# Prompt attention, one head at a time or two: scores, transposed weights and one eviction in shared banks

## The chip, the cores and the metric

The kernel runs on one core of a Trainium2 chip. The metric is device time in microseconds, the median of several executions. The engines are TensorE (PE; its weight loads are shown as PEld), VectorE (DVE), ScalarE (ACT), GpSimd (POOL) and SyncE (SP), which issues most of the transfers.

## The reference, cut to what matters

One inference step of a one-layer decoder: 1024 prompt tokens and 8 sample tokens go through gated branches (dilated window attention A, a convolution B, attention into 256 memory tokens M) and a channel mixer that retrieves experts. The change touches the prompt's part of A and M:

```python
# A: three head groups (window, dilation) = (128,1), (512,4), (2048,16), four heads each
s = jnp.einsum('brnqhd,brnkhd->brnhqk', qb, kk) * (HEAD_DIM ** -0.5)
s = jnp.where(mask[None, None, :, None], s, -jnp.inf)      # band of the window, blocks of 128
p, lse = softmax_lse(s)
o = jnp.einsum('brnhqk,brnkhd->brnhqd', p, vv)
...
# M: four heads, 256 memory tokens
s = jnp.einsum('bshd,bmhd->bhsm', qm, mk) * (HEAD_DIM ** -0.5)
p = jax.nn.softmax(s, axis=-1)
return jnp.einsum('bhsm,bmhd->bshd', p, mv)
```

All is float32; the outputs are the prompt's and the samples' rows and new cache rows.

## The kernel before, in words

The program prepares the memory keys and values, then runs `front` and `tail` for the first half of the prompt (512 tokens and the 8 samples), again for the second half, and last the dense expert stage `peer_dense`, beside which `peer_gather` fetches the experts of the last three token blocks by indirect DMA (L981). The dense stage begins near 1900 us.

Inside `front(hf, ...)` the projections write queries, keys and values to scratch in DRAM. A pool `mix` then holds everything from attention to the gated merge. For each of three groups and four packs of 128 queries (L357 to L388) the loads of queries, keys and values of this pack (and, where there is one, of the pack before) go to tiles `ld`. With a previous pack a head has 256 keys (`nk`), else 128. Per head: TensorE transposes keys and query into slot `t0` (L380), ScalarE evicts them to `kq` (L382), and `unit` does the rest. Memory attention (L420 to L439) calls the same `unit`, always with 256 keys. There are 24 packs of window attention (15 with 256 keys a head, 9 with 128) and 8 blocks of memory attention, so 128 calls of `unit`: 92 with 256 keys and 36 with 128.

`unit` does, for one head: a score matmul into slot `t1` (L319; it shows as two instructions, since the matmul is float32), a masked reduction on VectorE (L321, output S and the negated maximum), an exponential on ScalarE with its sum (L325), transposes of S into slot `t2` (L328), one eviction to ST by ScalarE (L330), and matmuls with the values into the head's columns of `po` (L332). The slots `t0`, `t1`, `t2` are one PSUM bank each (512 float32 a partition), with one buffer. S and ST are tiles of 256 columns in two buffers, `kq` has two.

In the first half alone, `sample_scores` (L390) reduces rows of the caches with VectorE (L405), and `sample_mix` (L441) multiplies cached values. Both load tiles of 128 x 512 float32 (256 KB) into a ring `sld` of eight buffers: keys at L396, broadcast queries at L400, values at L529. All these loads, attention's and the weights' go through SP's queue in one order.

The convolution of the first half runs 30 taps a channel block on VectorE (L575). Gates (L645) and the convolution's input (L559) are the bulk of TensorE's work here.

No order is written by hand. A planner takes the instructions in program order as priorities, with a simulated time line, and lays down one order for each engine and its queue; on the chip each engine keeps that order and waits at semaphores.

Of the kernel before, what the change touches and what calls it, by code (L numbers as in the profile page):

```python
# [9 lines left out]
F32 = mybir.dt.float32  # L10
# [6 lines left out]
OP = mybir.AluOpType  # L17
# [4 lines left out]
P = 128  # L22
# [24 lines left out]
def peer_trunk(tc, I, O):  # L47
# [11 lines left out]
    with contextlib.ExitStack() as es:  # L59
# [198 lines left out]
        def front(hf, keep, wp):  # L258
# [53 lines left out]
            with tc.tile_pool(name=f"mix{hf}", bufs=1) as mx, banks(f"mix{hf}"):  # L312
                LD = 10 if hf == 0 else 6


                def unit(qT, kT, nk, vs, mask, po, h, negm, den, name):

                    pS = t_tile(f"pS_{name}", 1)
                    nc.tensor.matmul(pS[:, :nk], qT, kT, start=True, stop=True)  # L319
                    S = mx.tile([P, 256], F32, tag="S", bufs=2, name=f"S_{name}")  # L320
                    nc.vector.tensor_tensor_reduce(  # L321
                        out=S[:, :nk], in0=pS[:, :nk], in1=mask, scale=-SCALE, scalar=BIG,
                        op0=OP.add, op1=OP.min, accum_out=negm,
                    )
                    nc.scalar.activation(S[:, :nk], S[:, :nk], AF.Exp, scale=-1.0, bias=negm, accum_out=den)  # L325
                    pT = t_tile(f"pT_{name}", 2)
                    for j in range(nk // P):
                        nc.tensor.transpose(pT[:, j * P : (j + 1) * P], S[:, j * P : (j + 1) * P], ident)  # L328
                    ST = mx.tile([P, 256], F32, tag="ST", bufs=2, name=f"ST_{name}")
                    nc.scalar.copy(ST[:, :nk], pT[:, :nk])  # L330
                    for j in range(nk // P):
                        nc.tensor.matmul(  # L332
                            po[:, h * P : (h + 1) * P], ST[:, j * P : (j + 1) * P], vs[j][:, h * P : (h + 1) * P],
                            start=j == 0, stop=j == nk // P - 1,
                        )

                def ld_tile(name):
                    return mx.tile([P, 520], F32, tag="ld", bufs=LD, name=name)

                def sld_tile(name):  # L340
                    return mx.tile([P, 512], F32, tag="sld", bufs=8, name=name)


                def rows_of(scr, g, pk, hh, c0, c1):
# [12 lines left out]
                for g in range(3):  # L357
                    for pk in range(4):
                        nm = f"{hf}{g}{pk}"

                        def ld(scr, which, hh, pp, cc, nm=nm, g=g):
                            t = ld_tile(f"w{which}{nm}")
                            nc.sync.dma_start(t[:, :512], rows_of(scr, g, pp, hh, cc, cc + 512))
                            return t

                        prev = prev_of(g, pk)
                        q = ld(qscr, "q", hf, pk, 512 * g)
                        ks = [ld(kscr, "kp", prev[0], prev[1], 0)] if prev else []
                        ks.append(ld(kscr, "ko", hf, pk, 0))
                        vs = [ld(vscr, "vp", prev[0], prev[1], 0)] if prev else []  # L370
                        vs.append(ld(vscr, "vo", hf, pk, 0))
                        nk = P * len(ks)
                        mask = masks[:, 1 if g == 2 else 0, 256 - nk : 256]
                        po = o_tile(f"wo{nm}")
                        ao = mx.tile([P, 520], F32, tag="ao", bufs=2, name=f"wao{nm}")
                        for h in range(4):
                            hs = slice(h * P, (h + 1) * P)
                            pt = t_tile(f"wT{nm}{h}", 0)
                            for j, src in enumerate(ks + [q]):
                                nc.tensor.transpose(pt[:, j * P : (j + 1) * P], src[:, hs], ident)  # L380
                            kq = mx.tile([P, 384], F32, tag="kq", bufs=2, name=f"kq{nm}{h}")
                            nc.scalar.copy(kq[:, : nk + P], pt[:, : nk + P])  # L382
                            unit(
                                kq[:, nk : nk + P], kq[:, :nk], nk, vs, mask, po, h,
                                ao[:, 512 + h : 513 + h], ao[:, 516 + h : 517 + h], f"w{nm}{h}",
                            )
                        nc.scalar.copy(ao[:, :512], po)
                        nc.sync.dma_start(rows_of(oscr[g], g, pk, hf, 0, 520), ao)  # L388
# [31 lines left out]
                for c0, n, row, rb in blocks[:4]:  # L420
# [1 line left out]
                    nc.sync.dma_start(qt[:, :512], qscr[row : row + n, 1536:2048])  # L422
                    po = o_tile(f"mo{hf}{c0}")
                    nm = small.tile([P, 8], F32, tag="nmd", name=f"mnmd{hf}{c0}")
                    for h in range(4):
                        pt = t_tile(f"mqT{hf}{c0}{h}", 0)
                        nc.tensor.transpose(pt[:, :P], qt[:, h * P : (h + 1) * P], ident)
                        kq = mx.tile([P, 384], F32, tag="kq", bufs=2, name=f"mqTs{hf}{c0}{h}")
                        nc.scalar.copy(kq[:, :P], pt[:, :P])
                        unit(  # L430
                            kq[:, :P], kTm[:, h, :], 256, (vm[:, 0, :], vm[:, 1, :]), zmask, po, h,
                            nm[:, h : h + 1], nm[:, 4 + h : 5 + h], f"m{hf}{c0}{h}",
                        )
                    nc.vector.reciprocal(nm[:, 4:8], nm[:, 4:8])
                    a = mx.tile([P, 520], F32, tag="ao", bufs=2, name=f"ma{hf}{c0}")
# [810 lines left out]
```

## Time and profile before

| | us |
|---|---|
| median of 3 runs | 3703.09 (3703.05 to 3704.65) |
| the profiled execution | 3695.24 |
| its span, first to last instruction | 3693.1 |
| TensorE busy | 3429.9 (93%) |
| VectorE busy | 2899.1 (78%) |
| ScalarE busy | 1499.6 (41%), 3519 instructions |

The rows further down come from this one execution. A row of a stage gives the busy time of each engine inside it and the mean granted clock of TensorE as a part of full speed (1.00 is 2.4 GHz; 0.5 would be 1.2 GHz all the time). A row of a wait names the waiting engine and line, the one that released it, the sum of the idle time, how often, and the longest.

### The profile page before, as it was taken

How to read it: one execution, taken by the hardware profiler on the slowest of the kernel's cores; microseconds unless marked ns; L12 is line 12 of the kernel's file. 1: busy time of each engine (PE TensorE's matmuls, PEld its weight loads, DVE VectorE, ACT ScalarE, POOL GpSimd, SP SyncE). 2: the span in 40 equal slices, each digit the busy share in tenths (PEclk: the TensorE clock that was granted, in tenths of full speed). 3: DMA queues.
4: the chain of work that ended last, by engine and by line, in shares of the span. 5: the costliest groups of instructions: out<-in, count | busy, mean ns of one | idle time of the engine just before them, and what ended most of it. 6: DMA issues, size and time to landing. Idle time of an engine off the chain costs nothing.

```text
span 3693.1 us, 55182 instructions
## 1 busy us (share of the span) xinstructions
PE 3429.9 (93%) x19969; PEld 3011.5 (82%) x19969; DVE 2899.1 (78%) x6275; ACT 1499.6 (41%) x3519; POOL 565.7 (15%) x398
## 2 busy tenths in 40 slices
PE   8987999898889989887899999999999999999998
PEld 6766989697677778676798888888989888898987
DVE  4358555499998656779988888887988888798988
ACT  6553552235755554344443333332333333233332
POOL 0000000000000000000012323322323332233332
PEclk9997999999999999998799999999999999999999
DMA  5467455423355546753668988888988988888987
GB/s 180 136 199 259 154 184 183 154 86 119 103 186 189 177 157 211 246 188 131 224 233 314 338 312 330 310 318 309 336 328 324 342 315 304 308 327 318 334 329 279
DMA packets 338454, 902.09 MB, mean 244 GB/s; under 512 B 32588, under 2 KB 140276, under 8 KB 285436
## 3 DMA queue, kind: packets, MB, share of 16 engines
q1 hardware_dynamic: 281732, 487.49, 39.7%
q0 software_dynamic: 56448, 411.07, 29.2%
q8 instruction: 157, 2.57, 0.3%
q14 instruction: 117, 0.96, 0.1%
HBM read 804.09 MB, written 94.83 MB: 243 GB/s over the span
## 4 chain that ended last, share of the span: by engine, by line
PE 31%; issue 30%; DVE 14%; DMA 13%; POOL 11%; ACT 2%; SPq 0%; POOLq 0%; DVEq 0%; ACTq 0%
POOL uv L981 11%; DMA uv<-in_uv,idxB 4%; PE pg L175 2%; PE pg L174 2%; PE pg L176 2%; PE pG L1057 2%; PE pG L1056 2%; DMA vr<-in_v_tab 1%; PE p_q L175 1%; PE p_q L176 1%; DMA wko<-kscr 1%; PE p_q L174 1%; DMA uv<-in_uv,idxS 1%; PE pa L174 1%; PE pa L176 1%
## 5 line engine op out<-in xcount | busy, mean ns | idle before, releaser
L981 POOL DMA_INDIRECT uv<-in_uv,idxB x384 | 555.8, 1448 | 1553.2 <-DVE gacc L995 1226.1
L174 PE MATMUL pa<-h2Ah,uh 128*128 128x320 f32 x2048 | 633.7, 310 | 2.2 <-ACT uh L158 2.2
L176 PE MATMUL pa<-h2Ah,ul 128*128 128x320 f32 x2048 | 631.9, 310 | 2.3 <-DVE ul L159 2.2
L175 PE MATMUL pa<-h2Al,uh 128*128 128x320 f32 x2048 | 633.2, 309 | 0.0
L985 DVE CUSTOM_DVE_ANT_0 uv<-uv,gh 128x1024 f32<-128x1024 f32 x392 | 478.5, 1222 | 138.2 <-DMA uv<-in_uv,idxB 119.9
L174 PE MATMUL pv<-vh,hh 128*128 128x512 f32 x1280 | 480.5, 396 | 44.3 <-ACT vh L158 28.4
L995 DVE SCALAR_TENSOR_TENSOR gacc<-uv,av,gacc 128x1024 f32<-128x1024 f32 x392 | 502.5, 1282 | 17.5 <-ACT av L993 12.6
L175 PE MATMUL pv<-vl,hh 128*128 128x512 f32 x1280 | 505.2, 395 | 9.3 <-DVE vl L159 9.3
L176 PE MATMUL pv<-vh,hl 128*128 128x512 f32 x1280 | 499.9, 393 | 0.0
L174 PEld LDWEIGHTS pa<-h2Ah,uh 128*128 128x128 f32 x2048 | 385.7, 188 | 6.9 <-ACT uh L158 2.4
L176 PEld LDWEIGHTS pa<-h2Ah,ul 128*128 128x128 f32 x2048 | 385.1, 188 | 5.4 <-DVE ul L159 2.8
L175 PEld LDWEIGHTS pa<-h2Al,uh 128*128 128x128 f32 x2048 | 385.4, 188 | 3.3 <-issue 0.9
L158 ACT CAST vh<-vr 128x512 fp32r<-128x512 f32 x256 | 157.2, 619 | 422.0 <-DMA vr<-in_v_tab 238.1
L174 PEld LDWEIGHTS pv<-vh,hh 128*128 128x128 f32 x1280 | 242.7, 190 | 99.0 <-ACT vh L158 40.0
L175 PEld LDWEIGHTS pv<-vl,hh 128*128 128x128 f32 x1280 | 243.6, 190 | 61.0 <-DVE vl L159 12.9
L176 PEld LDWEIGHTS pv<-vh,hl 128*128 128x128 f32 x1280 | 243.4, 190 | 50.0
L981 POOL DMA_INDIRECT uv<-in_uv,idxS x8 | 9.2, 1149 | 1556.3 <-ACT co L739 1513.2
L159 DVE TENSOR_TENSOR vl<-vr,vh 128x512 fp32r<-128x512 f32 x256 | 175.6, 688 | 77.0 <-ACT vh L158 76.5
L174 PE MATMUL pg<-hTh,wh_g 128*128 128x260 f32 (+1 forms) x576 | 192.9, 335 | 0.0
L175 PE MATMUL pg<-hTl,wh_g 128*128 128x260 f32 (+1 forms) x576 | 192.4, 334 | 0.0
L176 PE MATMUL pg<-hTh,wl_g 128*128 128x260 f32 (+1 forms) x576 | 192.3, 334 | 0.0
L990 ACT ACTIVATE av<-av 128x2 f32<-128x2 f32 x196 | 39.9, 204 | 375.3 <-DVE av L985 374.8
(558 smaller groups left out, 7651.3 us busy)
## 6 DMA issues: line engine op xcount, KB each, us to landing
ur<-in_uT SPq DMA_DIRECT2D x128, 512.0 KB
vr<-in_v_tab SPq DMA_DIRECT2D x256, 256.0 KB
gscr<-stg SPq DMA_DIRECT2D x20, 2048.0 KB
Gt<-gscr SPq DMA_DIRECT2D x32, 1280.0 KB
wr_g<-in_w_col SPq DMA_DIRECT2D x48, 512.0 KB
wr_q<-in_w_in SPq DMA_DIRECT2D x24, 512.0 KB
wr_u<-in_w_col SPq DMA_DIRECT2D x16, 512.0 KB
wr_pq<-in_w_col SPq DMA_DIRECT2D x16, 512.0 KB
```

Of the source, the lines that this page charges most:

```text
L158: nc.scalar.copy(hi, raw)
L159: nc.vector.tensor_tensor(lo, raw, hi.bitcast(F32), op=OP.subtract)
L174: nc.tensor.matmul(out, ah, bh, start=start, stop=False)
L175: nc.tensor.matmul(out, ah, bl, start=False, stop=False)
L176: nc.tensor.matmul(out, al, bh, start=False, stop=stop)
L981: nc.gpsimd.indirect_dma_start(out=uv, out_offset=None, in_=I["uv"], in_offset=bass.IndirectOffsetOnAxis(ap=col, axis=0),)
L985: nc.vector.tensor_tensor_reduce(out=uv[:, 0:D], in0=uv[:, 0:D], in1=h2, scale=1.0, scalar=0.0, op0=OP.mult, op1=OP.add, accum_out=av[:, s ...
L990: nc.scalar.activation(av, av, AF.Gelu_apprx_tanh)
L995: nc.vector.scalar_tensor_tensor(acc, uv[:, D:], av[:, j : j + 1], acc, op0=OP.mult, op1=OP.add)
L1056: nc.tensor.matmul(pG[:, q], o2[:, a, :, q], wh[:, a, :, q], start=True, stop=False)
L1057: nc.tensor.matmul(pG[:, q], o2[:, a, :, q], wl[:, a, :, q], start=False, stop=True)
```

## The change

`unit` becomes `pair`, for two heads. One tile of `t1` holds both heads' scores side by side, one tile S and one ST of 512 columns hold both heads, one tile of `t2` takes all transposes (two or four), and one eviction moves them. The query and key tiles of a head are made by a function that `pair` calls for each head (`window_qk`, `memory_qk`), so the transposes and the eviction to `kq` now stand inside the loop over the two heads. The score matmul, the reduction and the exponential stay one for each head. The transposes of both heads follow the second head's exponential in the program. The ring `sld` has seven buffers instead of eight.

```diff
-                def unit(qT, kT, nk, vs, mask, po, h, negm, den, name):
+                def pair(qkT, nk, vs, mask, po, h0, negm, den, name):
 
                     pS = t_tile(f"pS_{name}", 1)
-                    nc.tensor.matmul(pS[:, :nk], qT, kT, start=True, stop=True)
-                    S = mx.tile([P, 256], F32, tag="S", bufs=2, name=f"S_{name}")
-                    nc.vector.tensor_tensor_reduce(
-                        out=S[:, :nk], in0=pS[:, :nk], in1=mask, scale=-SCALE, scalar=BIG,
-                        op0=OP.add, op1=OP.min, accum_out=negm,
-                    )
-                    nc.scalar.activation(S[:, :nk], S[:, :nk], AF.Exp, scale=-1.0, bias=negm, accum_out=den)
+                    S = mx.tile([P, 512], F32, tag="S", bufs=2, name=f"S_{name}")
                     pT = t_tile(f"pT_{name}", 2)
-                    for j in range(nk // P):
+                    ST = mx.tile([P, 512], F32, tag="ST", bufs=2, name=f"ST_{name}")
+                    for q in range(2):
+                        qT, kT = qkT(h0 + q)
+                        nc.tensor.matmul(pS[:, q * nk : (q + 1) * nk], qT, kT, start=True, stop=True)
+                        nc.vector.tensor_tensor_reduce(
+                            out=S[:, q * nk : (q + 1) * nk], in0=pS[:, q * nk : (q + 1) * nk], in1=mask, scale=-SCALE,
+                            scalar=BIG, op0=OP.add, op1=OP.min, accum_out=negm(h0 + q),
+                        )
+                        nc.scalar.activation(
+                            S[:, q * nk : (q + 1) * nk], S[:, q * nk : (q + 1) * nk], AF.Exp, scale=-1.0,
+                            bias=negm(h0 + q), accum_out=den(h0 + q),
+                        )
+                    for j in range(2 * nk // P):
                         nc.tensor.transpose(pT[:, j * P : (j + 1) * P], S[:, j * P : (j + 1) * P], ident)
-                    ST = mx.tile([P, 256], F32, tag="ST", bufs=2, name=f"ST_{name}")
-                    nc.scalar.copy(ST[:, :nk], pT[:, :nk])
-                    for j in range(nk // P):
-                        nc.tensor.matmul(
-                            po[:, h * P : (h + 1) * P], ST[:, j * P : (j + 1) * P], vs[j][:, h * P : (h + 1) * P],
-                            start=j == 0, stop=j == nk // P - 1,
-                        )
+                    nc.scalar.copy(ST[:, : 2 * nk], pT[:, : 2 * nk])
+                    for q in range(2):
+                        hs = slice((h0 + q) * P, (h0 + q + 1) * P)
+                        for j in range(nk // P):
+                            js = slice(q * nk + j * P, q * nk + (j + 1) * P)
+                            nc.tensor.matmul(po[:, hs], ST[:, js], vs[j][:, hs], start=j == 0, stop=j == nk // P - 1)
...
-                    return mx.tile([P, 512], F32, tag="sld", bufs=8, name=name)
+                    return mx.tile([P, 512], F32, tag="sld", bufs=7, name=name)
...
-                        for h in range(4):
+                        def window_qk(h, nm=nm, ks=ks, q=q, nk=nk):
                             hs = slice(h * P, (h + 1) * P)
                             pt = t_tile(f"wT{nm}{h}", 0)
...
+                            return kq[:, nk : nk + P], kq[:, :nk]
+
+                        for h0 in (0, 2):
+                            pair(
+                                window_qk, nk, vs, mask, po, h0, lambda h, ao=ao: ao[:, 512 + h : 513 + h],
+                                lambda h, ao=ao: ao[:, 516 + h : 517 + h], f"w{nm}{h0}",
                             )
```

Memory attention is rewritten in the same way with `memory_qk`.

## Rows read from the trace of the kernel before

**Rows 1.** The page's first part: engines' busy time, share of the span, instructions.

```profile
PE 3429.9 (93%) x19969; PEld 3011.5 (82%) x19969; DVE 2899.1 (78%) x6275; ACT 1499.6 (41%) x3519; POOL 565.7 (15%) x398
```

**Rows 2.** Busy time by stage: us, engines busy (instructions), PE clock, DMA share, GB/s.

```profile
240.00:360.00 120.00, 92.95 (x544) 78.41 (x543) 99.90 (x471) 45.28 (x132) 0.00 (x0) 0.81 0.88 289
360.00:490.00 130.00, 128.70 (x1050) 126.34 (x1051) 69.10 (x156) 74.34 (x216) 0.00 (x0) 1.00 0.48 146
...
1260.00:1340.00 80.00, 64.33 (x347) 51.24 (x344) 43.93 (x75) 38.07 (x75) 0.00 (x0) 0.87 0.40 142
1340.00:1480.00 140.00, 136.95 (x845) 118.26 (x844) 84.98 (x163) 72.28 (x171) 0.00 (x0) 0.98 0.59 200
...
1900.00:3694.00 1794.00, 1731.16 (x9568) 1566.46 (x9567) 1517.14 (x1979) 567.31 (x1305) 547.87 (x378) 0.99 0.87 319
```

**Rows 3.** Score matmuls of window attention, first half, second half: count, ns, first and last start.

```profile
L319 PE MATMUL pS_w<-kq x96: 270/275/796, 244.8 to 432.5; 128*128 128x128 f32 x72, 128*128 128x256 f32 x24
...
L319 PE MATMUL pS_w<-kq x96: 377/379/716, 1054.0 to 1362.1; 128*128 128x256 f32 x96
```

**Rows 4.** Waits of TensorE, 240 to 500 us: waiter, releaser, us, times, longest.

```profile
PE pS_w L319 <- DVE wao L321: 20.1, 13, 5.7
...
PE pT_w L328 <- ACT S_w L325: 0.9, 2, 0.6
PE mo L332 <- ACT ST_m L330: 0.5, 1, 0.5
```

**Rows 5.** The same of the second half, 1080 to 1480 us.

```profile
PE wT L380 <- DMA wkp<-kscr: 17.2, 5, 7.9
...
PE wo L332 <- ACT ST_w L330: 2.0, 4, 0.9
...
PE pT_w L328 <- ACT S_w L325: 0.5, 1, 0.5
```

**Rows 6.** Groups of evictions, 240 to 1480 us: line, operation, shapes, count | busy, mean ns | idle.

```profile
L330 ACT COPY ST_w<-pT_w 128x256 f32<-128x256 f32 x60 | 22.5, 375 | 18.7 <-PE pT_w L328 18.0
...
L387 ACT COPY wao<-wo 128x512 f32<-128x512 f32 x24 | 14.0, 585 | 8.9 <-PE wo L332 8.9
...
L330 ACT COPY ST_m<-pT_m 128x256 f32<-128x256 f32 x32 | 12.0, 376 | 24.0 <-PE pT_m L328 23.7
...
L330 ACT COPY ST_w<-pT_w 128x128 f32<-128x128 f32 x36 | 9.7, 269 | 7.1 <-PE pT_w L328 6.9
```

**Rows 7.** Waits of VectorE, 240 to 500 us.

```profile
DVE skw L405 <- DMA sqw<-qscr: 12.8, 4, 7.6
...
DVE S_m L321 <- PE pT_m L328: 3.8, 1, 3.8
...
DVE skm L405 <- DMA sqm<-qscr: 2.5, 3, 1.7
...
DVE S_w L321 <- PE pT_w L328: 1.6, 2, 0.9
```

**Rows 8.** Time line around 343 us: start, us, engine, line, operation [idle before, releaser].

```profile
343.61 0.29 DVE L405 CUSTOM_DVE_ANT_0 skw<-skw,sqw 128x128 f32<-128x128 f32 x1 [7.56 <-DMA sqw<-qscr]
...
345.13 0.28 DVE L321 CUSTOM_DVE_ANT_0 S_w<-pS_w,c_masks 128x128 f32<-128x128 f32 x1
...
345.48 0.79 PE L319 MATMUL pS_w<-kq 128*128 128x128 f32 x2 [5.70 <-DVE wao L321]
```

**Rows 9.** Waits of SP's DMA queue, 240 to 360 us.

```profile
SPq L396 <- DVE s_allm L405: 7.0, 7, 2.1
...
SPq L396 <- DVE s_allw L405: 4.6, 4, 1.8
```

**Rows 10.** Waits of TensorE in the dense stage, 1900 to 3694 us.

```profile
PE pv L174 <- ACT vh L158: 28.4, 11, 5.4
PE pv L174 <- DVE dacc L1124: 12.9, 4, 7.4
PE pv L175 <- DVE vl L159: 9.3, 8, 4.1
```

More of the change, by code (lines that the diff above doesn't have):

```diff
@@ L382, in front @@
                             nc.scalar.copy(kq[:, : nk + P], pt[:, : nk + P])
-                            unit(
-                                kq[:, nk : nk + P], kq[:, :nk], nk, vs, mask, po, h,
-                                ao[:, 512 + h : 513 + h], ao[:, 516 + h : 517 + h], f"w{nm}{h}",
+                            return kq[:, nk : nk + P], kq[:, :nk]
[3 more added lines that the diff above has]
+                                lambda h, ao=ao: ao[:, 516 + h : 517 + h], f"w{nm}{h0}",
                             )
@@ L424, in front, with memory_qk @@
                     nm = small.tile([P, 8], F32, tag="nmd", name=f"mnmd{hf}{c0}")
-                    for h in range(4):
+                    def memory_qk(h, qt=qt, c0=c0):
                         pt = t_tile(f"mqT{hf}{c0}{h}", 0)
@@ L429, in front @@
                         nc.scalar.copy(kq[:, :P], pt[:, :P])
-                        unit(
-                            kq[:, :P], kTm[:, h, :], 256, (vm[:, 0, :], vm[:, 1, :]), zmask, po, h,
-                            nm[:, h : h + 1], nm[:, 4 + h : 5 + h], f"m{hf}{c0}{h}",
+                        return kq[:, :P], kTm[:, h, :]
+                    for h0 in (0, 2):
+                        pair(
+                            memory_qk, 256, (vm[:, 0, :], vm[:, 1, :]), zmask, po, h0,
+                            lambda h, nm=nm: nm[:, h : h + 1], lambda h, nm=nm: nm[:, 4 + h : 5 + h], f"m{hf}{c0}{h0}",
                         )
```

## The prediction

> **What bounds the kernel now.** I read the engine shares first [rows 1], then the span by stage [rows 2], then where the changed code runs [rows 3] and who waits for whom there [rows 4, 5], and last the groups of its evictions [rows 6]. TensorE is busy for 93% of the span. After 1900 us, half of the span and none of it touched by the change, it is busy 1731 of 1794 us. So the question for an edit in the prompt attention is how much TensorE idle time it creates or takes away before 1900 us; the rest follows behind.
>
> The changed code runs twice. The window heads' scores lie between 244.8 and 432.5 us in the first half and between 1054.0 and 1362.1 us in the second [rows 3], memory attention behind them, each time mixed by the planner with gate and convolution matmuls, which fill TensorE when attention has to wait. The stages differ. From 240 to 360 us TensorE is busy 93 of 120 us at a mean granted clock of 0.81; VectorE is busy 100 of 120 us, with convolution taps, the sample rows' scores and attention's score reductions in one queue. From 360 to 490 us TensorE is full (128.7 of 130 us at clock 1.00). In the second half, TensorE is idle for 16 of the 80 us from 1260 to 1340 us and nearly full on both sides of that [rows 2].
>
> Who ends these waits decides what the change can win. In the first half 20.1 us of TensorE's waiting is a score matmul (L319) held until VectorE has reduced the scores of the head before (L321); the waits on evictions are small [rows 4]. In the second half the largest, 17.2 us, is on loads of the previous keys [rows 5].
>
> **The change part by part.**
>
> One eviction for two heads. Before, there are 128 evictions at L330: 92 of 256 columns (60 and 32) at 375 to 376 ns and 36 of 128 columns at 269 ns. After, 46 pairs evict 512 columns and 18 pairs evict 256. An eviction of 512 columns from PSUM stands at L387 with 585 ns [rows 6]. ScalarE saves 46 x (2 x 0.375 - 0.585) = 7.6 us and 18 x (2 x 0.269 - 0.375) = 2.9 us, 10.5 us in all. ScalarE is busy 45 of 120 us and 74 of 130 us in the stages of the first half, and 72 of 140 us from 1340 us on [rows 2]: this lies beside other work, and I cost it at nothing for the end. Its cover is TensorE's queue of gate matmuls; without it the gain could be the 10.5 us at most.
>
> Fewer handshakes of TensorE with ScalarE. TensorE waited for the exponential before the transposes or for the evicted weights before the last matmul for 0.9 + 0.5 us in the first half and 2.0 + 0.5 us in the second, eight waits, 3.9 us [rows 4, 5]. Half as many meetings: -2.0 us, between 0 and -3.9. The same edit adds a wait. The four transposes of a pair now need the second head's exponential, and behind them in TensorE's queue stands whatever the planner put there. Only 2 + 1 heads of 128 waited at this place, 0.47 us each. If all 64 pairs did, that would be 30 us; with gate matmuls to put ahead, I take nothing.
>
> Scores sharing a bank. The second head's score matmul writes the other half of the tile that VectorE is reading for the first head. In the trace each score waits for the reduction before it through the one buffer of that slot: 20.1 us in 13 waits [rows 4]. If the new form let it go ahead, half of these waits, those inside a pair, would end: -10 us. If the planner orders accesses by whole banks, it is the same chain and 0. I take 0, because the program still writes matmul, reduction, exponential, matmul in this order. The Trainium skill (PSUM — Partial Sum Buffer, section "PSUM bank collisions raise a hardware error") says that two engines must not touch one bank in the same partitions at once, even in other columns, and that software has to hold them apart. By that rule the whole 20.1 us stays; without it the sum would be 10 us lower. The trace agrees as far as it goes, since every score of one slot waits for its reader, but no row shows two halves of one bank in use.
>
> Wider score and weight tiles. Two buffers now cover four heads. VectorE waited for transposes to free the old ones for 1.6 + 3.8 us [rows 7], on an engine that then has other work; 0 at the end, down to -5.4 if none of that were covered.
>
> One buffer fewer for the sample loads. These eight buffers hold the cache rows and broadcast queries that VectorE reads at L405, queued on SP between attention's own loads and the weights. VectorE waited 12.8 + 2.5 us for them, in seven waits [rows 7], and SP's issues at L396 waited 7.0 + 4.6 us for a buffer [rows 9]. What follows is visible once in full [rows 8]: VectorE stands 7.56 us until a query tile lands, the reduction of a head's scores stands behind that in its queue, and the next score on TensorE waits 5.70 us for it, so 0.75 of VectorE's wait reaches TensorE. In that stage the transfers are the limit (DMA share 0.88, 289 GB/s [rows 2]), so a shorter reach costs little: scaled by 8/7, the 15.3 us grow by 2.2, of which 0.75 gives +1.6 us. Below, 0. Above, each of the seven waits as long as the longest of its kind, 4 x 7.6 + 3 x 1.7 = 35.5 us, +20.2 on VectorE and +15.2 us at the end. Behind SP's longer waits stand weight loads; none of TensorE's waits in that stage names one, and I add nothing.
>
> The count of matmuls, transposes, reductions and exponentials stays. Sum: -2.0 + 1.6 = -0.4 us.
>
> The profiled execution took 3695.24 us, 2.1 us around its span of 3693.1, and lies 7.9 us below the median of 3703.09. On the profiled execution the sum gives 3694.8 us; on the median 3702.7 us. That is no change: below about 0.2%, 7.4 us, a measurement of this kernel can't be told from none.
>
> **What the sum can't hold.** The planner orders the whole program anew when instructions are joined, since it works with a simulated time line. Each wait can be dealt again, in the dense stage too, where TensorE waits 28.4 + 12.9 + 9.3 = 50.6 us for values just converted or sums just read [rows 10]. A fifth of that is 10 us in either direction, more than my sum.
>
> **The rivals.**
>
> Faster, by the scores: the new interleaving lets the 20.1 us shrink. For it speaks that this is the largest TensorE wait in the changed code and that two heads in flight give the planner more to put ahead; against it, that the reduction stands in VectorE's queue behind the same taps, and VectorE is busy 100 of 120 us. Half of it gone gives 3702.7 - 10 = 3692.7 us; all of it and all handshakes, 3703.1 - 20.1 - 3.9 = 3679.1 us. The low clock of that stage (0.81) is an extra: fewer gaps would give some of it back.
>
> Slower, by the sample buffers: with seven, the loads come later, VectorE stops more often at L405, and attention's reductions behind it hold TensorE. For it speaks the chain of [rows 8]; against it, that waits of VectorE of this kind were only seven and that DMA is full whatever the depth. At the upper bound 3702.7 - 1.6 + 15.2 = 3716.3 us. It decides the sign once VectorE's added waiting passes (7.4 + 2.0) / 0.75 = 12.5 us.
>
> The change doesn't do what it says: evictions stay at 128 in number. The program leaves no room for that; I give it nothing.
>
> **How the numbers follow.** No measurable change, 3702.7 us: 0.42, because the priced terms nearly cancel and lie away from the path. Faster by scores or a lucky order: 0.33. Slower by the sample buffers, by transposes waiting for a second exponential or by an unlucky order: 0.25. The cases hold both signs, so the range takes in most of both: low 3681, where almost all waits of the scores and the handshakes go, high 3720, the sample bound of 3716.3 with some pairs' waits for the second exponential (eight at 0.47 us) on top. The likeliest case alone spans 3695.7 to 3710.5.
>
> **What would show it.** ScalarE's instructions fall from 3519 to 3455, with 46 evictions near 0.585 us and 18 near 0.375 us at the new line; TensorE's and VectorE's counts stay. If I am right, TensorE still waits about 20 us for reductions between 240 and 500 us, its waits on exponentials and evictions stay below 4 us, VectorE's waits for sample queries stay within a few us of 15.3, and the dense stage begins and ends within 7 us of before. A fall of the score waits to 10 us or less shows the faster rival; more than 28 us of VectorE's waiting at L405, with score waits grown beside it, shows the slower one. A dense stage longer or shorter by over 7 us would mean that the planner's new order, and none of the priced terms, decided.

## The result, and the profile after

The changed kernel takes 3726.31 us (median of six runs, 3718.08 to 3739.49) against 3703.07 us for the kernel before in the same comparison: ratio 1.0057, 95% interval 1.0034 to 1.0081. That is 21 us slower and 6 us above the predicted range. The profiled execution took 3718.08 us, with a span of 3715.8 us (before 3693.1).

The page's first part after the change answers to [rows 1].

```profile
PE 3424.2 (92%) x19969; PEld 3009.9 (81%) x19969; DVE 2904.0 (78%) x6275; ACT 1491.7 (40%) x3453; POOL 564.1 (15%) x398
```

The work is the same: TensorE's and VectorE's counts have not moved, and TensorE is even busy for 5.7 us less. So the 22.7 us more of span, and these 5.7, are idle time of TensorE. To find where they lie I put marks at the first matmul of each stage: po1a (last output projection, "last tail"), tr_A (first transpose of the dense stage) and the 998th of the 9984 matmuls of the dense products, tiles `pa` and `pv` ("first tenth"). The first tr_A stands at 1800.3 us in the kernel before: the dense stage begins there and not near 1900 us, as the description ahead of the prediction has it. The next rows are busy time by stretch of the changed kernel; the columns are those of [rows 2].

```profile
240.00:360.00 120.00, 88.42 (x552) 76.23 (x551) 100.80 (x473) 45.86 (x124) 0.00 (x0) 0.84 0.89 292
360.00:490.00 130.00, 127.25 (x1030) 124.88 (x1029) 67.73 (x154) 70.21 (x193) 0.00 (x0) 0.98 0.46 141
1555.40:1806.80 251.40, 195.98 (x1284) 175.33 (x1285) 222.10 (x786) 105.56 (x176) 9.18 (x8) 0.88 0.52 183
1806.80:2035.10 228.30, 204.88 (x1136) 185.21 (x1135) 196.41 (x454) 84.44 (x154) 38.87 (x28) 0.92 0.74 263
2035.10:3680.00 1644.90, 1589.85 (x8834) 1444.48 (x8834) 1396.79 (x1817) 526.84 (x1210) 510.27 (x352) 0.98 0.87 320
```

The same last tail and first tenth in the kernel before:

```profile
1555.00:1800.30 245.30, 198.19 (x1283) 177.84 (x1284) 218.87 (x779) 104.61 (x172) 9.03 (x7) 0.89 0.52 182
1800.30:2012.00 211.70, 198.89 (x1135) 180.14 (x1134) 184.09 (x445) 82.62 (x148) 28.46 (x22) 0.94 0.74 262
```

Read the fourth row of after against the second of before. The same 1135 or 1136 matmuls take 228.3 us instead of 211.7. TensorE is idle for 23.4 us instead of 12.8, and its matmuls are busy 6.0 us longer at a mean granted clock of 0.92 instead of 0.94. VectorE does 12.3 us more in that stretch, and GpSimd issues 28 gathers instead of 22. The last tail is 6.1 us longer. Both stretches hold only code that the change does not touch. From the 998th matmul to the end it is 1681.1 us before and 1680.7 after. The attention stages together changed by nothing in this pair of traces: the first half (up to its own output projection) is 6.3 us longer, and what lies from there to the last tail is 6.3 us shorter.

TensorE's waits from 240 to 500 us answer to [rows 4], with waiter, releaser, us, times, longest:

```profile
PE pS_w L324 <- DVE wao L325: 27.6, 15, 5.0
...
PE mo L340 <- ACT ST_m L335: 0.7, 1, 0.7
...
PE wo L340 <- ACT ST_w L335: 0.3, 1, 0.3
```

From 1080 to 1480 us they answer to [rows 5]:

```profile
PE wT L385 <- DMA wkp<-kscr: 14.9, 7, 3.7
...
PE pT_w L334 <- ACT S_w L329: 2.7, 4, 0.7
PE wo L340 <- ACT ST_w L335: 1.5, 3, 0.7
```

VectorE's waits for sample queries, 240 to 500 us, answer to [rows 7] (L413 is the line that was L405):

```profile
DVE skw L413 <- DMA sqw<-qscr: 9.8, 3, 7.6
...
DVE skm L413 <- DMA sqm<-qscr: 2.0, 2, 1.7
```

The groups of evictions answer to [rows 6]: line, operation, shapes, count, busy us and mean ns, idle before.

```profile
L335 ACT COPY ST_w<-pT_w 128x512 f32<-128x512 f32 x30 | 17.6, 586 | 5.5 <-PE pT_w L334 4.9
...
L335 ACT COPY ST_m<-pT_m 128x512 f32<-128x512 f32 x16 | 9.3, 578 | 3.4 <-PE pT_m L334 3.4
L335 ACT COPY ST_w<-pT_w 128x256 f32<-128x256 f32 x18 | 6.8, 376 | 2.2 <-PE pT_w L334 2.0
```

These views say that no priced term grew by more than the 7.5 us of the reductions (27.6 for 20.1), with nothing left of it at the last tail, and that the loss is elsewhere.

**What happens where the dense stage starts.** Each block of values is split into a high part, copied by ScalarE (`vh`, L158), and a low part, subtracted by VectorE (`vl`, L159), before TensorE can multiply it. The next two rows are VectorE's part, called value splits here, in the first 100 us after the first tr_A, before and then after (duration in ns, first and last start in us):

```profile
L159 DVE TENSOR_TENSOR vl<-vr,vh x9: 671/685/693, 1853.9 to 1894.7; 128x512 fp32r<-128x512 f32 x9
```

```profile
L159 DVE TENSOR_TENSOR vl<-vr,vh x6: 683/684/693, 1871.1 to 1903.8; 128x512 fp32r<-128x512 f32 x6
```

Nine splits became six, and the first comes 64.3 us after the first tr_A instead of 53.6. The sixth comes 10.7 us later as well (97.0 and 86.3 us), so all of the delay has come in by the first. On VectorE the top-k of the last blocks and the one-hots of the gates stand ahead of them. From the first tr_A to the first split, before and then after:

```profile
1800.30:1853.90 53.60, 43.92 (x295) 41.40 (x294) 52.26 (x220) 24.08 (x39) 0.00 (x0) 0.79 0.74 243
```

```profile
1806.80:1871.10 64.30, 47.64 (x287) 42.94 (x286) 63.50 (x271) 31.17 (x45) 0.00 (x0) 0.78 0.59 197
```

VectorE is busy for 52.3 of 53.6 us and then for 63.5 of 64.3, with 271 instructions in place of 220. TensorE is idle there for 16.7 us in place of 9.7, which is 7.0 of the 10.6 us that the first tenth adds. But its waits hardly name the splits themselves. The longest of the first tenth, with the one on a split, before and then after:

```profile
PE pG L1057 <- DVE oh L1051: 5.1, 3, 2.4
PE pv L174 <- DVE dacc L1124: 2.5, 1, 2.5
...
PE pv L175 <- DVE vl L159: 0.6, 1, 0.6
```

```profile
PE pv L174 <- ACT vh L158: 5.5, 2, 4.9
PE pa L174 <- ACT ge L1113: 4.6, 2, 3.5
PE pG L1067 <- DVE oh L1060: 4.4, 2, 2.6
```

After, no wait on `vl` is in the list. What came in are waits on ScalarE's half of the values and on the gelu of the stage (`ge`), neither of which stood in the list before. So the splits mark how far VectorE has come; they are not what TensorE waits for by name.

The gathers' products come in earlier behind the splits: from the first tr_A to the 30th value split VectorE has spent 94 us on gathers (84 before). That early work on gathers is not needed at the end. The last rows are the products of the gathers over the whole span, before and then after:

```profile
L995 DVE SCALAR_TENSOR_TENSOR gacc<-uv,av,gacc x392: 1268/1282/1316, 1533.9 to 3685.8; 128x1024 f32<-128x1024 f32 x196
```

```profile
L1006 DVE SCALAR_TENSOR_TENSOR gacc<-uv,av,gacc x392: 1264/1280/1287, 1544.3 to 3690.2; 128x1024 f32<-128x1024 f32 x196
```

Before, the last one starts 7.3 us ahead of the end of the span, after 25.6 us ahead: the gathers run ahead of TensorE, which ends last by itself.

### The profile page after: what moved, and what is told of

The parts are those of the page before. It is cut to its first block, busy times and chain, and to the rows that moved or that the text cites. A ratio compares the mean times of both kernels' runs of the same rounds, so it can differ in the third digit from the quotient of the medians.

```text
span 3715.8 us, 54968 instructions
## 1 busy us (share of the span) xinstructions
PE 3424.2 (92%) x19969; PEld 3009.9 (81%) x19969; DVE 2904.0 (78%) x6275; ACT 1491.7 (40%) x3453; POOL 564.1 (15%) x398
## 4 chain that ended last, share of the span: by engine, by line
PE 35%; issue 21%; DVE 13%; DMA 12%; POOL 7%; ACT 2%; SPq 0%; POOLq 0%; DVEq 0%; ACTq 0%
POOL uv L992 7%; DMA uv<-in_uv,idxB 4%; PE pa L176 2%; PE pa L174 2%; PE pa L175 2%; PE pv L174 2%; PE pv L175 2%; PE pv L176 2%; PE pg L175 2%; PE pg L174 2%; PE pg L176 2%; DMA vr<-in_v_tab 2%; PE pG L1068 1%; PE pG L1067 1%; DMA wko<-kscr 1%
## 5 line engine op out<-in xcount | busy, mean ns | idle before, releaser
L174 PE MATMUL pv<-vh,hh 128*128 128x512 f32 x1280 | 476.8, 397 | 57.0 <-DVE dacc L1135 33.3
L158 ACT CAST vh<-vr 128x512 fp32r<-128x512 f32 x256 | 157.5, 619 | 446.5 <-DMA vr<-in_v_tab 232.0
L159 DVE TENSOR_TENSOR vl<-vr,vh 128x512 fp32r<-128x512 f32 x256 | 175.2, 687 | 95.8 <-ACT vh L158 95.7
L992 POOL DMA_INDIRECT uv<-in_uv,idxS x8 | 10.5, 1318 | 1571.4 <-DMA th<-gtscr 1523.6
L158 ACT CAST uh<-ur 128x1024 fp32r<-128x1024 f32 x128 | 134.3, 1049 | 169.3 <-PE pa L175 125.0
```

What stands on the lines that cost most here:

```text
L158: nc.scalar.copy(hi, raw)
L159: nc.vector.tensor_tensor(lo, raw, hi.bitcast(F32), op=OP.subtract)
L174: nc.tensor.matmul(out, ah, bh, start=start, stop=False)
L992: nc.gpsimd.indirect_dma_start(out=uv, out_offset=None, in_=I["uv"], in_offset=bass.IndirectOffsetOnAxis(ap=col, axis=0),)
```

## The experiments

The question after this was what sent the dense stage into another order, and whether pairs cost anything of themselves. There are three theories, numbered as in the expectations (the quoted texts, written before each run). Theory 1: any such edit makes the planner lay down another order of the dense stage, and that order costs the time. Theory 2: pairs cost time where they run. Theory 3: the missing eighth sample buffer costs time.

### One part alone: the ring of seven

The kernel before with only this line changed:

```diff
-                    return mx.tile([P, 512], F32, tag="sld", bufs=8, name=name)
+                    return mx.tile([P, 512], F32, tag="sld", bufs=7, name=name)
```

> The kernel before with one edit: the ring of sample loads has seven buffers, attention stays one head at a time. The planner's order of the dense stage comes out the same, instruction for instruction, as in the changed kernel (0 of 10190 TensorE rows moved, against 698 moved to the kernel before). Theory 1, the time goes in the re-dealt order of the last tail and the dense stage: slower by 15 to 25 us, with stages up to 1555 us within 5 us of before. Theory 2, attention's pairs hold TensorE longer: within 7 us of before. Theory 3, late sample loads: slower, but in the first half, with VectorE's waits at L405 above 28 us and the convolution's normalisation late by over 10 us.

Measured: 3719.17 us (3715.11 to 3729.63), ratio 1.0058, interval 1.0037 to 1.0079. That is the loss of the whole change, with attention one head at a time. The planned order of TensorE's queue in the dense stage (10190 rows) is the changed kernel's, row by row, where 698 rows stand elsewhere in the kernel before. The traces agree: from the first tr_A on, TensorE's, VectorE's, ScalarE's and GpSimd's instructions run in the same order in both. Its first tenth:

```profile
1805.70:2033.40 227.70, 203.41 (x1135) 183.28 (x1134) 195.87 (x454) 84.49 (x154) 37.55 (x28) 0.92 0.74 263
```

227.7 us, as after. But VectorE's waits for sample queries in the first half are 11.2 + 2.2 us (15.3 before), so a scarce supply did not do it.

### The other part alone, in the second half

Pairs only for `hf == 1`, where no sample loads exist, with a ring of eight.

```diff
+                TWO = hf == 1
...
-                        for h in range(4):
+                        for h in range(0 if TWO else 4):
...
+                        for h0 in (0, 2) if TWO else ():
+                            pair(
```

> Pairs of heads in the second half of the prompt alone; the first half keeps one head at a time and the ring of eight. The dense stage's order lies near that of the changed kernel (116 of 10190 TensorE rows moved, 675 to the kernel before). Theory 1, the dense order: slower by 10 to 25 us. Theory 2, pairs cost time themselves: about half of the loss, 8 to 14 us, and it shows between 1045 and 1460 us. Theory 3, sample loads: 0, since the ring is not used there.

Measured: 3709.83 us, ratio 1.0024, interval 1.0006 to 1.0042. The dense order is 116 rows from the changed kernel's and 675 from the one before; the first tenth takes 229.8 us. So the slow start comes without the ring as well. The total alone does not tell the theories apart: it is 7.9 us slower, below the 10 to 25 us of theory 1 and at the edge of the 8 to 14 us of theory 2. The place does, in part: in the profiled execution (3722.17 us, 12 us above the median) the first tenth is 18.1 us longer than before and the second-half attention 3.4 us (541.3 us, 537.9 before).

### The dense order held by a fence

A barrier of all engines ahead of the gathers and the dense stage keeps the planner from mixing what lies on both sides. It costs time, so one kernel of each form has it:

```diff
+        tc.strict_bb_all_engine_barrier()
         base = tc.cur_priority
         tc.cur_priority = gprio
```

> The kernel before with a barrier of all engines ahead of the gathers and the dense stage. It is the base for the next run; by itself it costs what the gathers and the dense stage lose in overlap with the last tail, 10 to 80 us by every theory.

> The changed kernel with the same barrier; the dense order behind it is now nearly that of the kernel before with the barrier (96 of 9998 TensorE rows moved). Theory 1, the dense order: within 8 us of the other kernel with the barrier. Theory 2, attention's pairs, and theory 3, sample loads: slower than that one by 15 to 25 us, as without the barrier, since the loss lies ahead of it.

Measured: 3775.55 us one head at a time (ratio 1.0207, interval 1.0186 to 1.0228) and 3769.66 us in pairs (1.0198, 1.0176 to 1.0221). The dense orders differ in 96 rows. First tenths, one head and then pairs:

```profile
1872.40:2102.10 229.70, 190.40 (x1038) 172.63 (x1038) 172.57 (x226) 70.58 (x157) 65.24 (x44) 0.89 0.91 331
```

```profile
1867.00:2099.20 232.20, 190.99 (x1037) 172.56 (x1038) 172.38 (x226) 70.54 (x157) 63.38 (x44) 0.88 0.90 327
```

With the dense stage nearly the same in both, the change's 21 us loss is gone; the 5.9 us in favour of pairs are within the intervals. So pairs with the ring of seven do not lose time of themselves, up to these intervals. The first tenth behind the fence is as slow in both as in the changed kernel; what the fence shows is that the forms cost the same under nearly one order.

### Both kernels once more

No edit: one more profile of each, to see which differences by stage repeat.

> The kernel before once more, for a second profile. If the loss is a property of the planned order at the start of the dense stage, the stretch from the first transpose of the dense stage (tr_A) to its 998th matmul takes 212 us again, within 5, and the rest to the end 1681, within 8. If the first profile was a lucky one, that stretch takes 220 us or more here.

> The changed kernel once more, for a second profile. If the loss is a property of the planned order at the start of the dense stage, the stretch from tr_A to the 998th matmul takes 228 us again, within 5, and the rest 1681, within 8. If it was an unlucky profile, the stretch is nearer to 212.

Measured: 3695.77 and 3702.94 us. From the one to the other, the first half is 0.5 us longer (6.3 in the first pair of traces), the stretch up to the second-half attention 3.8 us shorter (1.8), the second-half attention 3.8 us shorter (4.5), the last tail 4.6 us longer (6.1), the first tenth 19.6 us longer (16.6) and the rest 9.0 us shorter (0.4). So the slow first tenth and the tail repeat, though these two executions are only 7.2 us apart, and the changed kernel's rest, 1670.7 us, lies outside the 8 us expected. The first half and the rest wander from one execution to the next: the fenced kernel before, with the same planned order up to the last tail, reached it at 1562.6 us where the plain one did at 1555.0.

### Pairs with the ring of eight

To give the eighth sample buffer back, ST gets one buffer instead of two.

```diff
-                    ST = mx.tile([P, 512], F32, tag="ST", bufs=2, name=f"ST_{name}")
+                    ST = mx.tile([P, 512], F32, tag="ST", bufs=1, name=f"ST_{name}")
...
-                    return mx.tile([P, 512], F32, tag="sld", bufs=7, name=name)
+                    return mx.tile([P, 512], F32, tag="sld", bufs=8, name=name)
```

> Pairs of heads in both halves with the ring of eight kept; the room comes from one buffer less of the evicted weights ST. The dense order is another one again (695 TensorE rows moved against the kernel before, 614 against the changed one). Theory 1, the order that the planner happens to deal: anything from 10 us faster to 25 us slower, and the difference sits in the last tail and the first tenth of the dense stage. Theory 2, pairs cost time: 15 to 25 us slower, before 1555 us. Theory 3, the ring of seven cost time by late loads: within 7 us of before.

Measured: 3688.95 us, ratio 0.9964, interval 0.9943 to 0.9986: faster than both kernels. The second-half stage, from the first matmul of its convolution's input to the last tail, before, after and here:

```profile
1017.10:1555.00 537.90, 491.51 (x2814) 408.50 (x2814) 396.86 (x763) 268.01 (x603) 6.26 (x6) 0.94 0.55 190
```

```profile
1022.00:1555.40 533.40, 488.31 (x2813) 404.59 (x2813) 395.82 (x762) 264.67 (x567) 5.11 (x4) 0.95 0.55 190
```

```profile
1014.60:1536.80 522.20, 484.33 (x2814) 402.85 (x2814) 391.39 (x752) 262.77 (x569) 5.12 (x4) 0.96 0.56 194
```

The 15.7 us that this stage is shorter than before carry the gain, in a place that none of the three theories had named. The dense stage is a third order (695 rows from the one before, 614 from after), whose first tenth is slow too, 224.4 us. How much of the 15.7 us belongs to the buffers and how much to a kind order of that stage no run separates.

### Pairs in the first half

Pairs for `hf == 0` with the ring of seven, one head in the second half (`TWO = hf == 0`).

> Pairs in the first half alone, with the ring of seven; the second half one head at a time. The dense order is a fourth one (530 TensorE rows moved against before, 427 against the changed kernel). Theory 1: anything from 10 us faster to 25 us slower, with the difference in the last tail and the first tenth of the dense stage. Theories 2 and 3, pairs or late sample loads in the first half: 15 us slower or more, present at 655 us already.

Measured: 3721.4 us, ratio 1.0056, interval 1.0031 to 1.0081; first tenth 224.8 us. Each half alone meets the slow start. Whether the two halves' losses add up to more than the whole (1.0056 and 1.0024 against 1.0057) can't be told within the intervals. In the profiled execution (11 us above the median) the first half is 9.3 us longer than before, less than the 15 us of theories 2 and 3, and VectorE waits 13.1 us there for sample queries (15.3 before), which speaks against theory 3. But the last tail and the first tenth (+3.6 and +13.1 us) hold only half of its 37 us; 17.4 us lie in the rest. Between theories 1 and 2 this run alone does not decide.

### Four forms chosen by their planned order

The planned order can be read before a kernel runs. Each of the next four was chosen for what it puts on VectorE ahead of the value splits. Their expectations call the figures 75, 76 and 85 "gather instructions"; they are in truth the planner's estimate, in microseconds, of the gather work on VectorE up to the 30th value split. From the first tr_A on the traces show 84 us for before, 85 us for the three that were meant to be early, and 94 for the late one.

A ring of six, alone (`bufs=6` on the kernel before):

> The kernel before with a sample ring of six buffers instead of eight; attention stays one head at a time. Theory of the supply (fewer loads ahead hold VectorE and attention): the loss grows with each buffer taken, so two buffers cost about twice the 16.1 us of one, near 3735 us, and VectorE waits over 28 us for sample queries. Theory of the order (the ring acts only by making the planner deal the queues anew): this planned order puts less top-k and one-hot work on VectorE ahead of the first value splits of the dense stage than that of ring7_alone, about as little as the kernel before (76 gather instructions by the 30th value split, 75 before, 85 in ring7_alone), so the first tenth of the dense matmuls takes 208 to 218 us as before (227.7 in ring7_alone), and the whole lies between 3698 and 3710 us, faster than with seven buffers.

Measured: 3713.75 us, ratio 1.0029, interval 1.0016 to 1.0042. The next rows are its first half up to the first-half tail, and its first tenth; then the same first half before.

```profile
219.70:669.40 449.70, 390.27 (x3053) 357.01 (x3051) 277.89 (x930) 199.07 (x543) 0.00 (x0) 0.91 0.62 196
...
1817.90:2034.30 216.40, 198.81 (x1136) 180.58 (x1135) 188.30 (x449) 83.71 (x148) 34.76 (x24) 0.93 0.73 260
```

```profile
218.80:655.70 436.90, 384.68 (x3053) 352.04 (x3051) 277.23 (x930) 199.92 (x543) 0.00 (x0) 0.93 0.63 201
```

Its waits from 240 to 500 us, TensorE's and VectorE's:

```profile
PE pS_w L319 <- DVE wao L321: 28.4, 13, 5.4
...
DVE skw L405 <- DMA sqw<-qscr: 15.6, 5, 6.5
...
DVE skm L405 <- DMA sqm<-qscr: 4.6, 5, 2.4
```

The first tenth came as the order said, 216.4 us, and two buffers fewer did not cost twice as much as one: the medians say less (3713.75 against 3719.17 us), though the intervals touch. But the total missed its 3698 to 3710 us. The first half is 12.8 us longer in the profiled execution, which is the slowest of twelve, 12.9 us above their median (4.0 us of it can be wander: one_head_again, the same kernel as before, took 440.9 us for 436.9), with VectorE waiting 20.2 us for sample queries (15.3 before) and TensorE 28.4 us for reductions (20.1). So the chain of [rows 8] exists; at six buffers it may show, at seven it did not.

One buffer fewer for attention's own loads in the first half, nothing else:

```diff
-                LD = 10 if hf == 0 else 6
+                LD = 9 if hf == 0 else 6
```

> The kernel before with nine instead of ten buffers for attention's own loads in the first half; sample ring eight, one head at a time. Theory of the order: its planned dense order stands 113 rows from that of the changed kernel and 686 from the kernel before, with 85 gather instructions by the 30th value split; so the first tenth of the dense matmuls takes 225 to 231 us, the gathers end over 20 us ahead of the end, and the whole is 3715 to 3725 us, though neither pairs nor the sample ring are touched. Theory that pairs or the sample ring cost it: 3698 to 3708 us, with a first tenth near 210 us.

Measured: 3715.18 us, ratio 1.0032, interval 1.0019 to 1.0046. First tenth, and the value splits in the first 100 us after tr_A:

```profile
1802.70:2032.60 229.90, 204.45 (x1135) 185.54 (x1134) 194.69 (x455) 84.78 (x154) 33.07 (x26) 0.91 0.72 255
```

```profile
L159 DVE TENSOR_TENSOR vl<-vr,vh x6: 684/686/692, 1869.0 to 1901.8; 128x512 fp32r<-128x512 f32 x6
```

Six splits and 229.9 us, with neither pairs nor the sample ring touched. Its first half is not longer at all (432.3 us, 436.9 before).

The changed kernel with another dense order:

```diff
-                    return mx.tile([P, 512], F32, tag="sld", bufs=7, name=name)
+                    return mx.tile([P, 512], F32, tag="sld", bufs=6, name=name)
...
-                            kq = mx.tile([P, 384], F32, tag="kq", bufs=2, name=f"kq{nm}{h}")
+                            kq = mx.tile([P, 384], F32, tag="kq", bufs=3, name=f"kq{nm}{h}")
...
```

(The same in `memory_qk`.)

> The changed kernel, pairs in both halves, with a sample ring of six and three buffers for the evicted keys and queries (two before). Theory of the order: its planned order has the first value splits of the dense stage as early as the kernel before (76 gather instructions by the 30th value split), so the first tenth of the dense matmuls takes 208 to 218 us instead of 228.3, and the whole falls to 3692 to 3706 us. Theory of the pairs or of the supply: 3720 us or more, as in the changed kernel, since it pairs as much and has one sample buffer fewer still.

Measured: 3698.16 us, ratio 0.9984, interval 0.9972 to 0.9996. The same two views:

```profile
1802.20:2021.60 219.40, 199.71 (x1135) 180.95 (x1134) 189.01 (x451) 84.00 (x149) 34.12 (x24) 0.93 0.73 255
```

```profile
L159 DVE TENSOR_TENSOR vl<-vr,vh x9: 677/686/732, 1865.7 to 1900.9; 128x512 fp32r<-128x512 f32 x9
```

Nine splits again, and all of the loss is gone with pairs everywhere and one sample buffer fewer still. The first tenth is 1.4 us above what was expected, the whole inside it.

Pairs in the second half's window attention alone, ring of eight:

> Two heads at a time only in the window attention of the second half, memory attention one head at a time, sample ring eight. Theory of the order: the dense stage has the early value splits (76 gather instructions by the 30th of them), its first tenth takes 208 to 218 us, and the stage of second-half attention falls by 3 to 5 us as in the changed kernel: 3695 to 3705 us. If pairs in the second half cost time of themselves, as the 3709.8 us of pairs_second_half could be read: 3708 us or more.

Measured: 3699.64 us, ratio 0.9992, interval 0.9976 to 1.0008; first tenth 215.1 us, as expected. Its second-half stage did not fall by 3 to 5 us, but took 549.3 us in the profiled execution (537.9 before); that part missed. Its dense order is that of two_heads_other_order, row by row. Over all profiles the second-half stage took 522 to 534 us with pairs in both halves, 541.3 and 549.3 with pairs in the second alone, and 534.9 to 544.1 with one head there, so no cost or gain of pairs themselves is shown in it.

The table puts the kernels by their dense order. "Sixth split" is the start of the sixth value split after the first tr_A; all lengths are us of one profiled execution each, and the two kernels that ran twice have both.

| kernel | dense order | ratio | sixth split | first tenth | rest |
|---|---|---|---|---|---|
| before | B | 1 | 86.3, 85.8 | 211.7, 208.7 | 1681.1, 1679.7 |
| pairs_windows_second | Y | 0.9992 | 87.8 | 215.1 | 1670.8 |
| two_heads_other_order | Y | 0.9984 | 87.9 | 219.4 | 1667.3 |
| ring6_alone | own | 1.0029 | 89.2 | 216.4 | 1690.6 |
| pairs_first_half | own | 1.0056 | 92.4 | 224.8 | 1698.5 |
| pairs_ring8 | own | 0.9964 | 96.5 | 224.4 | 1673.3 |
| ring7_alone | A | 1.0058 | 96.5 | 227.7 | 1680.6 |
| after | A | 1.0057 | 97.0, 97.0 | 228.3, 228.3 | 1680.7, 1670.7 |
| pairs_second_half | near A | 1.0024 | 97.9 | 229.8 | 1676.9 |
| load_ring9_alone | near A | 1.0032 | 99.1 | 229.9 | 1676.3 |

Two things are shown by it. Order A costs 1.0057 to 1.0058 with either form of attention, order Y 0.9984 to 0.9992 with either. And a later sixth value split goes with a longer first tenth, nearly in one line through the ten. The first split would not sort them: it starts 62.1 to 66.3 us after the first tr_A in all but the kernel before. That the splits' place is what delays TensorE, rather than something that moves with it, is not shown: no run moved the splits alone, and TensorE's waits name other things. Nor does the first tenth carry everything: pairs_ring8 is the fastest with a slow one, and from after to two_heads_other_order it gives back 8.9 of some 27 us (ratios 1.0057 and 0.9984 of 3703 us). Between these two profiled executions another 13.4 us lie in the rest of the dense stage, though the second profile of the changed kernel makes that 3.4. TensorE's longest waits over the whole dense stage, after and then two_heads_other_order:

```profile
PE pv L174 <- DVE dacc L1135: 33.3, 4, 10.6
PE pv L174 <- ACT vh L158: 23.7, 7, 5.2
```

```profile
PE pv L174 <- ACT vh L158: 23.7, 6, 9.5
PE pv L174 <- DVE dacc L1135: 11.3, 3, 7.7
```

For the sums read at the end of a chunk (`dacc`) it waits 33.3 us (23.0 in two_heads_again) against 11.3 us (17.7 in pairs_windows_second, with the same order), and 12.9 before [rows 10]. But this is no loss against the kernel before: from the 998th matmul to the end TensorE is idle for 58.8 us before and 59.2 after, and for 45.8 us in two_heads_other_order. So in these profiles order Y is short there, and order A is not long.

## Why the prediction was wrong

**The step that failed** is "the rest follows behind" in the first part, and with it the figure that stood for it later: the planner's new order was named, put at a fifth of the waits of [rows 10], 10 us in either direction, and then taken as zero in the sum. The last tail (+6.1 and +4.6 us) and the first tenth (+16.6 and +19.6 us) make +22.7 and +24.2 us in the two pairs of traces. I looked for the room in the wrong place as well. [rows 10] lists the waits that the old order had left, and [rows 2] one row for everything after 1900 us, in which TensorE seems full; the dense stage begins 100 us earlier, and the last tail and the first half of the first tenth stood in no row. At the start of the dense stage top-k, one-hots, splits and gathers meet on VectorE, and a view of 1800 to 2012 us would have shown TensorE idle for 12.8 us at a clock of 0.94 there, and VectorE busy 184 of 212 us. A stage that an edit does not touch still had a term in the sum, and its size is not that of its present waits. The range ended at 3720 for the sample bound and held no case in which the order alone costs 20 us.

**The cause by itself:** the slower rival was there, but with the wrong price in front. Its mechanism, VectorE's longer waits for sample queries, did not come: 11.8 us after, 15.3 before, so the term of +1.6 us had the wrong sign in these traces. The buffer acted through the order: ring7_alone has the same loss with 13.4 us of these waits.

**Evictions:** right. 17.6 + 9.3 + 6.8 = 33.7 us at L335 against 44.2 us before [rows 6], the 10.5 us of the sum, at 586, 578 and 376 ns (585 and 375 predicted). ScalarE's instructions fell to 3453, by two more than the 64: the traces have 29 loads of ScalarE's function tables (ACT_TABLE_LOAD) in place of 31, as in ring7_alone, so this too came with the order. No run ties the 7.9 us less of ScalarE's busy time to the end.

**Handshakes:** the term of -2.0 us did not come. TensorE's waits on the exponential and the evicted weights are 0.7 + 0.3 + 2.7 + 1.5 = 5.2 us, 3.9 before. The waits on evictions are 2.5 us as before, although there are half as many evictions. Those on the exponential went in the first half (0.9 us before) and grew from 0.5 to 2.7 us in the second. That can be the added wait, which I put at nothing and which stayed small; ring7_alone waits 1.5 us there with one head at a time, so the order has a part in it. The forecast "below 4 us" was missed by 1.2.

**Scores sharing a bank:** right at 0 or a little worse. TensorE waits 27.6 us (23.9 in two_heads_again) for reductions, 20.1 and 21.2 before; the form does not decide it, since it is 19.1 us in pairs in pairs_ring8 and 28.4 us with one head in ring6_alone. In none of the 64 pairs does the second score begin before the first head's reduction has ended; the shortest gap is 63 ns. What the Trainium skill (PSUM — Partial Sum Buffer, section "PSUM bank collisions raise a hardware error") says, that software must keep two engines apart in one bank even in other columns, is what the trace shows this program do; no run here tried it otherwise.

**S and ST in wider tiles:** VectorE's waits for transposes, 1.6 + 3.8 us [rows 7], are gone from its list, and nothing at the end shows it.

**What would show it:** the last sentence of that part held. The dense stage began 6.5 us later and was 16.2 us longer (10.5 in the second pair), and the new order, not the priced terms, decided.

## What to carry to other kernels

Where a planner lays down the order of the whole program, the first question about a small edit is how much time lies in stages that it does not touch: read the crowded places of every engine there, and give the sum a term for a new order of the size that small edits have (here -0.4 to +0.6%). Before a cause is named, run an edit with the same new order and without the suspected cause, and the suspected cause with another order; a buffer count whose own waits do not grow serves for both. And if the untouched order is a good one, an edit has first to win back what losing it costs.

## What the runs showed that I had not expected

- One load buffer fewer (load_ring9_alone), with no stage of attention longer by over 2.0 us in its profile, costs 0.32% (interval 0.19 to 0.46), and six sample buffers (1.0029) cost no more than seven (1.0058).
- The start of the dense stage is tight on VectorE: the sixth value split 11 us later goes with a first tenth 17 to 20 us longer. Of the 16.6 us, 10.6 are idle time of TensorE and 6.0 are busy time of the same matmuls, at a granted clock of 0.92 in place of 0.94.
- GpSimd's gathers that come early are not given back: the last of their products starts 25.6 us ahead of the end in place of 7.3.
